# Output projection of a hybrid decoder layer by seven block products instead of eight, with the sums of weight blocks made in DRAM by adding transfers

## The chip, the cores and the metric

The kernel runs on one core of a Trainium2 chip. The metric is the device time in microseconds (us) of one execution; the median of 3 executions of the kernel before is 2147.32 us (2146.45 to 2153.07). Engines are named as in the profile: PE is TensorE's matmuls and PEld its weight loads, DVE is VectorE, ACT is ScalarE, POOL is GpSimd, SP is SyncE (here it only issues transfers).

## The reference

One decoder layer for 1024 tokens of width 2048: a norm, one input projection to 7776 columns, a group of gated-delta-rule heads and a group of sparse-attention heads that read its columns, and then the part that the change is about. The two groups' gated outputs are put side by side (2048 columns) and go through one output projection, with a residual add and a last norm:

```
o_a = rms_norm(o_a, gdn_norm_g[l]).reshape(b, t, GDN_W) * jax.nn.silu(gz)
...
o_b = dsa_sparse_attention(q_b, k_b, v_b, q_i, k_i, w_i, k_sel) * jax.nn.silu(az)
mixed = jnp.concatenate([o_a, o_b], axis=-1).astype(x.dtype) @ w_out[l]
x = x + mixed
...
return rms_norm(x, final_norm_g)
```

`mixed` is a product of a 1024 x 2048 matrix with a 2048 x 2048 matrix, in float32.

## The kernel before

Every large product is done in float32r from a high and a low part of each operand: three matmuls (high x high, high x low, low x high) for one product of tiles. A weight tile is loaded as float32 (`wraw`), rounded by ACT into `whi`, and the remainder is written to `wlo` by a subtract.

The order of work: a norm and transposition of x into 8 tiles `hT` (16 KB a partition each, 8 buffers of one tag); input projection slabs of 256 columns (`slab_cm`, banks `cm`, 192 matmuls of 512 columns each, 8 weight pieces of 256 KB a slab, `wlo` written by POOL at L195); beside the slabs run, as side work of lower priority, the indexer, the top-k search, attention (`attend`) and the delta rule. The slabs for k, q and v are followed by those for the gates (`proj_gate`), which write `szT` to DRAM; attention and the delta rule write `oT`. A list `per_piece` holds small functions; each weight piece 1 to 5 of a slab pops one and runs it behind the piece's split. In the kernel before the list holds 17 functions that make decay tables (`decay_units`).

The output projection comes last. For each half of the tokens (`hf`, 512 tokens), `mix` loads `oT` and `szT` for a k-tile of 128 rows, multiplies them (`mt`, L1233, DVE), rounds the product (L1234, ACT) and takes the remainder (L1238, DVE). Then for each 512 columns `c`, 16 weight pieces of 128 x 512 (`w_piece_k`, loaded on POOL's queue at L227, `wlo` by DVE at L232) are each used in 12 matmuls (4 token tiles x 3) into 4 banks `to` (L1309). The first half does 4 such column groups, the second 3; the last 512 columns of the second half go as two groups of 256 columns (`tm` at L244 and `tl` at L1336). `add_x` adds x to a finished bank (L1266), squares it with a running sum on ACT (L1270) and multiplies by the last norm's gain (L1272). `finish_rows` makes the row factor and scales and stores the rows. The tiles of this stage take over the 8 buffers of `hT` as the last gate slab lets them go.

Instructions are put in order by a scheduler that simulates a timeline, with priorities: weight pieces first (`P_W`), then evacuations and mixes (`P_EV`), side work (`P_SIDE`), matmuls of slabs last (`P_MM`). Each engine then runs its own list in that order, and so do the transfer queues of SP, POOL and ACT: an instruction that waits holds all behind it on its engine.

Of the kernel before, what the change touches and what calls it, by code (L numbers as in the profile page):

```python
# [22 lines left out]
P = 128  # L23
# [29 lines left out]
def hybrid_layer(ctx: ExitStack, tc, x, positions, attn_norm_g, w_in, conv_w, a_log, dt_bias,  # L53
# [139 lines left out]
    def w_split(whi, wlo, raw, ncol, eng):  # L193
        ins = S.activation(whi[:, :, :ncol], raw[:, :, :ncol], AF.Copy)  # L194
        eng.tensor_tensor(wlo[:, :, :ncol], raw[:, :, :ncol], whi[:, :, :ncol].bitcast(F32), op=ALU.subtract)  # L195
        return ins

    def w_piece(srcs, p, ncol, w2d, keep=False, into=None):

        with pri(P_W):  # L200
            raw = wp.tile([P, KPP, CG], F32, tag="wraw", name="wraw")
            o = 0
            for c0, n in srcs:
                (G if w2d is w_out else SP).dma_start(raw[:, :, o:o + n],
                                              w2d[p * KPP * P:(p + 1) * KPP * P, c0:c0 + n].rearrange("(k p) c -> p k c", p=P))
                o += n
# [8 lines left out]
            ins = w_split(whi, wlo, raw, ncol, V if w2d is w_out else G)  # L215
            if per_piece and 1 <= p <= 5:
                per_piece.pop(0)(ins)
        return whi, wlo

    last_w = []  # L220

    def w_piece_k(kt, c0):

        with pri(P_W):
            shape = [P, 2 * CG]
            raw = wp.tile(shape, F32, tag="wraw", name="wraw")
            G.dma_start(raw, w_out[kt * P:(kt + 1) * P, c0:c0 + 2 * CG])  # L227
# [3 lines left out]
            last_w[:] = [S.activation(whi, raw, AF.Copy),  # L231
                         V.tensor_tensor(wlo, raw, whi.bitcast(F32), op=ALU.subtract)]  # L232
# [891 lines left out]

    def decay_units():
# [3 lines left out]
        def load(c, g):  # L1129
            def fn(ins):  # L1130
                E[c, g] = gcp[0].tile([P, 4, P], F32, tag="gce", name="gce", bufs=2)
                SP.dma_start(E[c, g], gcrow[c * HEADS + 4 * g:c * HEADS + 4 * g + 4, :][None, :, :].to_broadcast([P, 4, P]))
            return fn

        def make(c, g):
            def fn(ins):
# [10 lines left out]
        def slot(n):  # L1147
            def fn(ins):
                if n < len(units):
                    load(*units[n])(ins)  # L1150
                if n > 0:
                    make(*units[n - 1])(ins)
# [10 lines left out]
    with tc.tile_pool(name="atp", bufs=1, reuse_waits="tile") as atp:  # L1163
        attention(atp, kvp)
# [36 lines left out]
    mtp = ctx.enter_context(tc.tile_pool(name="mtp", bufs=2, side="right", reuse_waits="tile"))  # L1201
# [6 lines left out]

    op = ctx.enter_context(tc.tile_pool(name="op", bufs=1, reuse_waits="tile"))

# [3 lines left out]
    ORDER = (4, 5, 6, 7, 0, 1, 2, 3)  # L1214
    mx = {}
    last_ox = [None]

    def mix(hf, q, ks, behind=None):

        tsl = slice(hf * HT, (hf + 1) * HT)  # L1220
        if (hf, q) not in mx:
            if hf == 1 and q in (2, 3):
                mx[hf, q] = op.tile([P, 4, 2, HT], F32R, name=f"mx1_{q}")
            else:
                mx[hf, q] = bigt(f"mx{q}", [P, 4, 2, HT], F32R)
        for k in ks:
            hi, lo = mx[hf, q][:, k, 0, :], mx[hf, q][:, k, 1, :]
            for t, src in ((hi, oT), (lo, szT)):
                ld = SP.dma_start(t.bitcast(F32), src[:, 4 * q + k, tsl])
                if last_ox[0] is not None:  # L1230
                    after(ld, last_ox[0])
            m = mtp.tile([P, HT], F32, tag="mt", name="mt", bufs=1)
            mul = V.scalar_tensor_tensor(m, hi.bitcast(F32), 0.5, lo.bitcast(F32), op0=ALU.mult, op1=ALU.mult)  # L1233
            rnd = S.activation(hi, m, AF.Copy)  # L1234
            if behind is not None:
                after(rnd, behind[0])
                after(mul, behind[1])
            V.tensor_tensor(lo, m, hi.bitcast(F32), op=ALU.subtract)  # L1238

    turn_k = itertools.count()  # L1240
    KTS = [p * KPP + k for p in ORDER for k in range(KPP)]
    fg = None
    for hf in range(2):
        NL = D - hf * CG
        with pri(P_EV):
            if hf == 0:
                for q in (2, 3, 0, 1):
                    mix(0, q, range(4 if q != 1 else 2))
            ys = [bigt(f"y{i}", [P, 2, D]) for i in range(2)]
            ss = gp.tile([P, 4, 5], F32, tag="oss", name="oss", bufs=2)  # L1250
            nss = {}
            if hf == 0:
                fg = bigt("fg", [P, D])
                SP.dma_start(fg, final_g[None, :].to_broadcast([P, D]))

        def m_ap(kt, part, sl):
            return mx[hf, kt // 4][:, kt % 4, part, slice(sl.start - hf * HT, sl.stop - hf * HT)]

        def add_x(ps, b0, nb, c0, c1):

            w = c1 - c0
            xr = op.tile([P, nb, w], F32, tag="ox", name="ox", bufs=2)
            t0 = (4 * hf + b0) * P
            last_ox[0] = SP.dma_start(xr, x[t0:t0 + nb * P, c0:c1].rearrange("(b p) c -> p b c", p=P))
            y = ys[b0 // 2][:, b0 % 2:b0 % 2 + nb, c0:c1]
            V.tensor_tensor(y, ps, xr, op=ALU.add)  # L1266
            for j in range(nb):
                jk = sdt("oj")
                n = nss.setdefault((b0 + j, c0), sum(k[0] == b0 + j for k in nss))
                S.activation(jk[:, :w], y[:, j, :], AF.Square, accum_out=ss[:, b0 + j, n:n + 1])  # L1270
            if c1 <= NL:
# [99 lines left out]
```

## Time and profile before

| | |
|---|---|
| median of 3 executions | 2147.32 us |
| profiled execution's own time | 2149.51 us |
| its span (first to last instruction) | 2147.7 us |
| mean granted TensorE clock | 0.992 of full speed |
| PE busy | 2079.6 us (97%) |
| DVE, ACT, POOL busy | 60%, 41%, 30% |

The time of an execution is its span and some 2 us around it. PE is busy nearly throughout, so a busy share by engine tells little by itself: what a stage lasts is read from stretches of the span, from the gaps of PE in them, and from the chain of waits.

### The profile page before, as it was taken

What the parts mean: (1) busy time and instruction counts of PE and PEld (TensorE: products, weight loads), DVE (VectorE), ACT (ScalarE), POOL (GpSimd) and SP (SyncE); (2) the same over time, 40 slices, a digit from 0 to 9 for tenths busy, and PEclk for the clock granted to TensorE, in tenths of its full rate; (3) what the DMA queues carried; (4) which work ended last, traced back from release to release, by engine and by line L of the source; (5) the groups of instructions that cost most, each with busy time, mean ns of one, the idle gap of its engine ahead of it and who ended that gap; (6) DMA issues with size and microseconds to landing.
All of it is one profiled execution on the core that took longest, in us unless ns stands there. A gap on an engine that the chain in (4) does not pass through costs nothing.

```text
span 2147.7 us, 30435 instructions
## 1 busy us (share of the span) xinstructions
PE 2079.6 (97%) x10529; PEld 1749.6 (81%) x10529; DVE 1298.4 (60%) x2798; ACT 872.0 (41%) x2054; POOL 642.2 (30%) x696
## 2 busy tenths in 40 slices
PE   7999999999999999999999998999999999999998
PEld 7888888877787788888888886778888887777888
DVE  8626766899999756555554479930453344445335
ACT  7425544433123555555544442122554323334223
POOL 6433334556532211222211122222322221121111
PEclk9999999999999999999999999999999999999999
DMA  6222223343224444222222242255665364556434
GB/s 190 72 74 77 74 77 79 110 129 118 86 73 113 142 116 120 81 77 85 76 63 72 70 104 59 78 163 164 182 181 147 103 235 132 168 162 230 134 120 159
DMA packets 263627, 252.08 MB, mean 117 GB/s; under 512 B 66688, under 2 KB 213552, under 8 KB 262896
## 3 DMA queue, kind: packets, MB, share of 16 engines
q1 hardware_dynamic: 210032, 188.25, 29.9%
q0 software_dynamic: 10240, 33.56, 5.1%
q10 hardware_dynamic: 43200, 28.32, 4.4%
q8 instruction: 83, 1.36, 0.3%
q14 instruction: 72, 0.59, 0.1%
HBM read 185.66 MB, written 64.39 MB: 116 GB/s over the span
## 4 chain that ended last, share of the span: by engine, by line
PE 51%; DVE 8%; DMA 5%; issue 2%; ACT 1%; SPq 1%; POOL 0%; DVEq 0%; ACTq 0%; POOLq 0%
PE cm L292 26%; PE to L1309 12%; PE lgp L148 3%; DVE ut L947 2%; PE po L148 2%; DVE mb L949 2%; PE pT L151 1%; DMA gcd<-gcrow 1%; DMA mx<-szT 1%; PE tl L1336 1%; PE tm L244 1%; PE ctok L151 1%; DVE cy L714 1%; DMA ox<-in_x_dram 1%; PE hh L923 0%
## 5 line engine op out<-in xcount | busy, mean ns | idle before, releaser
L292 PE MATMUL cm<-hT,whi 128*128 128x512 f32 (+1 forms) x3776 | 1205.6, 395 | 6.4 <-DVE sz L1121 5.7
L292 PEld LDWEIGHTS cm<-hT,whi 128*128 128x128 f32 (+1 forms) x3776 | 706.4, 188 | 151.0 <-DVE sz L1121 6.6
L292 PE MATMUL cm<-hT,wlo 128*128 128x512 f32 (+1 forms) x1888 | 746.5, 395 | 8.7 <-POOL wlo L195 8.7
L195 POOL TENSOR_TENSOR wlo<-wraw,whi 128x512 fp32r<-128x512 f32 (+1 forms) x248 | 337.3, 1361 | 902.6 <-ACT whi L194 840.3
L292 PEld LDWEIGHTS cm<-hT,wlo 128*128 128x128 f32 (+1 forms) x1888 | 355.6, 188 | 85.0 <-POOL wlo L195 14.3
L194 ACT ACTIVATE whi<-wraw 128x512 fp32r<-128x512 f32 (+1 forms) x256 | 158.7, 620 | 366.0 <-PE cm L292 252.6
L1309 PE MATMUL to<-whi,mx 128*128 128x512 f32 x896 | 279.8, 393 | 2.3 <-ACT whi L231 1.6
L1309 PEld LDWEIGHTS to<-whi,mx 128*128 128x128 f32 x896 | 167.9, 188 | 43.2 <-ACT whi L231 2.4
L664 DVE TENSOR_SCALAR_CACHE_REDUCE tj<-score,cand 128x384 bf16<-128x384 f32 (+2 forms) x198 | 187.1, 945 | 6.4
L1309 PE MATMUL to<-wlo,mx 128*128 128x512 f32 x448 | 174.7, 392 | 2.9 <-DVE wlo L232 2.9
L232 DVE TENSOR_TENSOR wlo<-wraw,whi 128x512 fp32r<-128x512 f32 x112 | 76.8, 690 | 143.1 <-ACT whi L231 143.0
L519 DVE SCALAR_TENSOR_TENSOR score<-rl,wi,score 128x512 f32<-128x512 f32 (+3 forms) x150 | 127.9, 862 | 29.5 <-ACT rl L511 22.8
L227 POOL DMA_DIRECT2D wraw<-in_w_out_dram x112 | 60.3, 539 | 252.4 <-DVE wlo L232 233.5
L231 ACT ACTIVATE whi<-wraw 128x512 fp32r<-128x512 f32 x112 | 70.1, 629 | 157.1 <-PE to L1309 124.8
L714 DVE SCALAR_TENSOR_TENSOR cy<-xr,convw,cy 128x512 f32<-128x512 f32 x144 | 118.4, 822 | 22.5 <-ACT cy L712 20.1
L832 DVE CUSTOM_DVE_ANT_0 lg<-lgp,mk 128x512 f32<-128x512 f32 (+3 forms) x96 | 53.1, 554 | 83.5 <-PE lgp L148 83.2
L1309 PEld LDWEIGHTS to<-wlo,mx 128*128 128x128 f32 x448 | 84.0, 188 | 22.4 <-DVE wlo L232 3.8
L851 DVE TENSOR_TENSOR pT<-pT 128x512 fp32r<-128x512 f32 (+1 forms) x80 | 49.7, 633 | 63.3 <-ACT pT L850 62.9
L511 ACT ACTIVATE rl<-isc 128x512 f32<-128x512 f32 (+1 forms) x105 | 59.0, 571 | 55.7 <-PE isc L148 30.2
L1121 DVE SCALAR_TENSOR_TENSOR sz<-sz,cm 128x512 f32<-128x512 f32 x32 | 21.7, 682 | 90.8 <-ACT sz L1120 90.2
L148 PE MATMUL lgp<-kT,qaT 128*128 128x512 f32 (+3 forms) x288 | 70.4, 353 | 3.9 <-ACT qaT L814 3.9
L148 PE MATMUL po<-pT,vv 128*128 128x256 f32 x432 | 72.7, 287 | 0.0
(282 smaller groups left out, 2671.1 us busy)
## 6 DMA issues: line engine op xcount, KB each, us to landing
wraw<-in_w_in_dram SPq DMA_DIRECT2D x232, 256.0 KB, 2.8
wraw<-in_w_out_dram POOLq DMA_DIRECT2D x128, 256.0 KB, 3.2
xt<-in_x_dram SPq DMA_DIRECT2D x32, 256.0 KB, 3.3
szT<-sz SPq DMA_DIRECT2D x32, 256.0 KB, 2.6
mx<-oT SPq DMA_DIRECT2D x32, 256.0 KB, 5.5
mx<-szT SPq DMA_DIRECT2D x32, 256.0 KB, 5.7
ox<-in_x_dram SPq DMA_DIRECT2D x30, 256.0 KB, 3.6
iqr<-iqT SPq DMA_DIRECT2D x48, 128.0 KB, 2.9
```

What stands on the lines that cost most here:

```text
L148: return anchored(PE.matmul(*a, **k))
L194: ins = S.activation(whi[:, :, :ncol], raw[:, :, :ncol], AF.Copy)
L195: eng.tensor_tensor(wlo[:, :, :ncol], raw[:, :, :ncol], whi[:, :, :ncol].bitcast(F32), op=ALU.subtract)
L227: G.dma_start(raw, w_out[kt * P:(kt + 1) * P, c0:c0 + 2 * CG])
L231: last_w[:] = [S.activation(whi, raw, AF.Copy), V.tensor_tensor(wlo, raw, whi.bitcast(F32), op=ALU.subtract)]
L232: V.tensor_tensor(wlo, raw, whi.bitcast(F32), op=ALU.subtract)]
L292: mms.append(PE.matmul(bank[:n, :], w[:, k, g * P:g * P + n], h_ap(kt, a, slice(h * HT, h * HT + HT)), start=(p == 0 and k == 0 and i == 0 ...
L511: S.activation(rl[:, :w], ps2[:, :w], AF.Relu)
L519: V.scalar_tensor_tensor(dst, r, w1, dst, op0=ALU.mult, op1=ALU.add)
L664: V.tensor_scalar(junk[:, :(b + 1) * P], score[b], cand[:, i:i + 1], 0.0, op0=op, op1=ALU.add, accum_out=cnt[:, i:i + 1])
L714: V.scalar_tensor_tensor(y, xr[:, j:j + HT], convw[:, j, ch:ch + 1], y, op0=ALU.mult, op1=ALU.add)
L1309: PE.matmul(banks[j], m_ap(KTS[m], a, slice((4 * hf + j) * P, (4 * hf + j + 1) * P)), ws[m][w], start=(m == 0 and i == 0), stop=(m == D // ...
```

## The change

Both matrices of the output projection are cut in four blocks: tokens in two halves (512), the inner dimension in two halves (1024), output columns in two halves (1024). Instead of eight products of blocks the changed kernel makes seven, from blocks and from sums or differences of blocks, and adds their results to the four blocks of the output in a fixed order (a form of Strassen's scheme). `wo(i, j)` are blocks of W_out; `RIGHT` lists the right-hand factor of each product.

Four of the right-hand factors are sums: `wsum1` to `wsum4`, 1024 x 1024 each, in DRAM. `block_sums` puts 32 functions in `per_piece`, behind those of `decay_units`. Each issues one transfer of 1 MB (256 rows) from POOL's queue, DRAM to DRAM: 16 plain copies and 16 that add to what is at the destination. They run behind weight pieces of the k and q slabs. A transfer that reads or adds to a slice waits for the transfer that wrote it.

The left-hand factors are made in SBUF (`factor_a`): mixes of one half, or differences of mixes (`m11`, `m21`, `m22`), split in a pair of high and low tiles; there are two sets of pairs, so a product's factor is made while the one before runs. `ms12` keeps one block in DRAM for later use. `take` evacuates a finished bank: up to two DVE adds from the bank, and adds of x and products with the gain on POOL (before, DVE did these). All w_out pieces are loaded on SP's queue (before on POOL's). A product has two column groups of 512, the first in the banks of `pj`, the second in those of the side work; 16 weight pieces, each in 12 matmuls as before: 192 matmuls a product.

```diff
-    def w_piece_k(kt, c0):
+    def w_out_piece(src):
...
-            G.dma_start(raw, w_out[kt * P:(kt + 1) * P, c0:c0 + 2 * CG])
+            SP.dma_start(raw, src)
...
+    def block_sums():
+
+        R = 256
+
+        def part(dst, src, add, r):
+            def fn(ins, low):
+                sl = slice(r * R, (r + 1) * R)
+                ld = G.dma_start(wsum[dst][sl], src[sl], accum_op=ALU.add) if add else G.dma_start(wsum[dst][sl], src[sl])
+                after(ld, low)
+            return fn
+        for dst, src, add in ((1, wo(0, 0), False), (3, wo(0, 1), False), (1, wo(0, 1), True), (3, wo(1, 1), True),
+                              (2, wsum[1], False), (2, wo(1, 1), True), (4, wsum[2], False), (4, wo(1, 0), True)):
+            for r in range(HC // R):
+                per_piece.append(part(dst, src, add, r))
...
+    def gated(i, k, hf, a, dst):
+
+        hi, lo = parts(i, k)
+        kt = k + KH * (1 - a)
+        for t, src in ((hi, oT), (lo, szT)):
+            SP.dma_start(t.bitcast(F32), src[:, kt, hf * HT:(hf + 1) * HT])
+        V.scalar_tensor_tensor(dst, hi.bitcast(F32), 0.5, lo.bitcast(F32), op0=ALU.mult, op1=ALU.mult)
+
+    def split(i, k, m):
+        hi, lo = parts(i, k)
+        S.activation(hi, m, AF.Copy)
+        V.tensor_tensor(lo, m, hi.bitcast(F32), op=ALU.subtract)
...
+    def factor_a(i, k):
+
+        if i == 0:
+            gated(0, k, 0, 0, m11[:, k, :])
+            split(0, k, m11[:, k, :])
+        elif i == 1:
+            gated(1, k, 1, 0, m21[:, k, :])
+            V.tensor_tensor(m11[:, k, :], m21[:, k, :], m11[:, k, :], op=ALU.subtract)
+            split(1, k, m11[:, k, :])
...
+        elif i == 4:
+            t = temp()
+            V.tensor_tensor(t, m21[:, k, :], m22[:, k, :], op=ALU.subtract)
+            split(4, k, t)
...
+    RIGHT = (wo(0, 0), wsum[3], wo(1, 0), wsum[2], wsum[1], wo(1, 1), wsum[4])
+
+    def with_x(hf, ch, j, cs, sub=False):
+
+        xr = stage.tile([P, 3 + HT], F32, tag="xr", name="ox", bufs=4)[:, 3:]
+        t0 = hf * HT + j * P
+        SP.dma_start(xr, x[t0:t0 + P, ch * HC + cs.start:ch * HC + cs.stop])
+        y = ys[hf, ch][:, j, cs]
+        G.tensor_tensor(y, y, xr, op=ALU.subtract if sub else ALU.add)
...
+    def gain(hf, ch, j, cs):
+        y = ys[hf, ch][:, j, cs]
+        G.tensor_tensor(y, y, fg[:, ch * HC + cs.start:ch * HC + cs.stop], op=ALU.mult)
+
+    def take(i, j, c, b):
+
+        cs = slice(c * 512, (c + 1) * 512)
+        a0, a1, y1, y2 = (t[:, j, cs] for t in (acc[0], acc[1], y11, y22))
+        if i == 0:
+            S.activation(a0, b, AF.Copy)
+        elif i == 1:
+            V.tensor_tensor(a1, b, a0, op=ALU.subtract)
+        elif i == 2:
+            V.tensor_tensor(y1, b, a0, op=ALU.add)
+            with_x(0, 0, j, cs)
+            square(0, 0, j, c)
+            gain(0, 0, j, cs)
...
+        elif i == 4:
+            V.tensor_tensor(y2, b, a1, op=ALU.add)
+            V.tensor_tensor(a0, b, a0, op=ALU.add)
+            with_x(1, 0, j, cs, sub=True)
+            with_x(1, 1, j, cs)
+            square(1, 1, j, c)
+            gain(1, 1, j, cs)
...
+    def products(i, banks, js, pieces, first, last):
+        for j in js:
+            for k, (whi, wlo) in pieces:
+                hi, lo = parts(i, k)
+                for n, (a, w) in enumerate(((hi, whi), (hi, wlo), (lo, whi))):
+                    PE.matmul(banks[j], a[:, j * P:(j + 1) * P], w, start=(k == first and n == 0), stop=(k == last and n == 2))
+
+    SP.dma_start(fg, final_g[None, :].to_broadcast([P, D]))
+    prepare_a(0)
+    prepare_a(1)
+    for i in range(7):
+        for c in range(2):
...
+                got.append((k, w_out_piece(RIGHT[i][k * P:(k + 1) * P, c * 512:(c + 1) * 512])))
+                if k != KH - 2:
+                    with pri(P_MM):
+                        products(i, banks, range(NT), got, 0, KH - 1)
+                    got = []
+            for j in range(NT):
...
+                with pri(P_EV):
+                    take(i, j, c, banks[j])
+        if i + 2 < 7:
+            prepare_a(i + 2)
```

Three places in the engines' orders. First POOL in the k slabs: before, between two `wlo` subtracts of the input weights stand only small copies for the convolution (`xr`, `halo`).

```order
L195 TENSOR_TENSOR wlo<-wraw,whi 128x512 [waits DMAHW5_49,Activation_49]
L710 COPY xr<-halo 128x3 [waits DVE_49,DMAHW2_49,PE_49,Pool_49]
L195 TENSOR_TENSOR wlo<-wraw,whi 128x512 [waits DMAHW2_49,Activation_49]
L195 TENSOR_TENSOR wlo<-wraw,whi 128x512 [waits DMAHW4_49,Activation_49]
L195 TENSOR_TENSOR wlo<-wraw,whi 128x512 [waits DMAHW0_49,Activation_49]
L195 TENSOR_TENSOR wlo<-wraw,whi 128x512 [waits DMAHW6_49,Activation_49]
```

Now an adding transfer (L1137) stands behind each of five pieces of a slab, with a wait on the earlier transfer to its slice (DMASW):

```order
L195 TENSOR_TENSOR wlo<-wraw,whi 128x512 [waits DMAHW5_49,Activation_49]
L1137 DMA wsum_4549<-in_w_out_dram 256x1024 [waits DMASW2_49]
L707 COPY xr<-halo 128x3 [waits DVE_49,DMAHW1_49,PE_49,Pool_49]
L195 TENSOR_TENSOR wlo<-wraw,whi 128x512 [waits DMAHW2_49,Activation_49]
L1137 DMA wsum_4549<-in_w_out_dram 256x1024 [waits DMASW3_49]
L195 TENSOR_TENSOR wlo<-wraw,whi 128x512 [waits DMAHW4_49,Activation_49]
L1137 DMA wsum_4551<-in_w_out_dram 256x1024 [waits DMASW4_49]
L195 TENSOR_TENSOR wlo<-wraw,whi 128x512 [waits DMAHW0_49,Activation_49]
L1137 DMA wsum_4551<-in_w_out_dram 256x1024 [waits DMASW5_49]
```

A `wlo` that stood directly behind another now stands behind a transfer that may wait. Second, DVE at the end of a column group of the output projection: before, one add from each bank, the gain, and mixes between weight pieces (L232).

```order
L1266 TENSOR_TENSOR y_16516<-to,ox 128x512 [waits PE_49] x2
L1272 TENSOR_TENSOR y_16516<-y_16516,fg 128x512 [waits DMAHW1_49,Activation_49]
L232 TENSOR_TENSOR wlo<-wraw,whi 128x512 [waits DMASW1_49,Activation_49]
L1272 TENSOR_TENSOR y_16516<-y_16516,fg 128x512 [waits Activation_49]
L1266 TENSOR_TENSOR y_16517<-to,ox 128x512 [waits DMAHW0_49,PE_49]
L232 TENSOR_TENSOR wlo<-wraw,whi 128x512 [waits DMASW2_49,Activation_49]
```

Now, at the end of the fifth product's first column group, two adds from each bank (L1337, L1338), one of which waits for POOL, and between the weight pieces (L229) the remainders of the next factor (L1264):

```order
L1337 TENSOR_TENSOR m_16470<-to,acc_16466 128x512 [waits PE_49]
L1338 TENSOR_TENSOR acc_16465<-to,acc_16465 128x512 [waits Pool_49]
L1337 TENSOR_TENSOR m_16470<-to,acc_16466 128x512 [waits PE_49]
L1338 TENSOR_TENSOR acc_16465<-to,acc_16465 128x512 [waits Pool_49]
L1337 TENSOR_TENSOR m_16470<-to,acc_16466 128x512 [waits PE_49]
L229 TENSOR_TENSOR wlo<-wraw,whi 128x512 [waits DMAHW3_49,Activation_49]
L1338 TENSOR_TENSOR acc_16465<-to,acc_16465 128x512 [waits Pool_49]
L229 TENSOR_TENSOR wlo<-wraw,whi 128x512 [waits DMAHW4_49,Activation_49]
L1264 TENSOR_TENSOR pr_16461<-m_16468,pr_16461 128x512 [waits PE_49,Activation_49]
L229 TENSOR_TENSOR wlo<-wraw,whi 128x512 [waits DMAHW5_49,Activation_49]
```

The gain has left DVE's list, and the second add and the wait for POOL have come in. Third, SP's queue in the same product: loads of x that wait for POOL (`ox`, L1305) now stand among the loads of weight pieces (L224), which were on POOL's queue before.

```order
L224 DMA wraw<-wsum_4550 128x512 [waits DMAHW4_49,DVE_49]
L1305 DMA ox<-in_x_dram 128x512 [waits DMAHW0_49,Pool_49]
L1305 DMA ox<-in_x_dram 128x512 [waits Pool_49]
L1305 DMA ox<-in_x_dram 128x512 [waits DMAHW2_49,Pool_49]
L224 DMA wraw<-wsum_4550 128x512 [waits DMAHW5_49,DVE_49]
L1305 DMA ox<-in_x_dram 128x512 [waits Pool_49]
L224 DMA wraw<-wsum_4550 128x512 [waits DMAHW6_49,DVE_49]
```

The sixth and seventh weight piece of the group are issued only when POOL has let go of an `ox` buffer.

## Rows read from the trace of the kernel before

**Rows 1.** The page, part 1: busy time of PE over the span.
```profile
PE 2079.6 (97%) x10529; PEld 1749.6 (81%) x10529; DVE 1298.4 (60%) x2798; ACT 872.0 (41%) x2054; POOL 642.2 (30%) x696
```
**Rows 2.** Busy time by stretch: the k and q slabs, the output projection in two parts.
```profile
core 0: us, PE busy (x) PEld busy (x) DVE busy (x) ACT busy (x) POOL busy (x), PEclk, DMA share, GB/s
570.00:960.00 390.00, 380.31 (x1934) 319.74 (x1933) 287.59 (x688) 179.03 (x500) 98.39 (x104) 0.99 0.37 103
1776.00:2091.00 315.00, 310.13 (x1339) 250.38 (x1339) 137.68 (x248) 100.61 (x183) 60.27 (x111) 1.00 0.50 159
2091.00:2138.50 47.50, 47.00 (x390) 46.35 (x388) 26.70 (x70) 18.21 (x40) 8.52 (x12) 1.00 0.43 148
```
**Rows 3.** Groups by line, 1776 to 2091: busy us, mean ns of one, idle time before.
```profile
L1309 PE MATMUL to<-whi,mx 128*128 128x512 f32 x892 | 278.5, 393 | 2.3 <-ACT whi L231 1.6 <-DVE sz L1121 0.6
L232 DVE TENSOR_TENSOR wlo<-wraw,whi 128x512 fp32r<-128x512 f32 x110 | 75.4, 690 | 143.1 <-ACT whi L231 143.0
L1266 DVE TENSOR_TENSOR y<-to,ox 128x512 f32<-128x512 f32 x25 | 16.7, 687 | 20.8 <-PE to L1309 15.7 <-DMA ox<-in_x_dram 5.1
L204 POOL DMA_DIRECT2D wraw<-in_w_out_dram x4 | 2.9, 720 | 8.3 <-DVE wlo L232 6.3 <-DVE wlo L195 2.0
```
**Rows 4.** Chain of waits, output projection: start us, length us, what.
```profile
1832.30 33.35 PE to L1309 x144
1968.60 121.91 PE to L1309 x528
2116.66 21.80 PE tl L1336 x185
```
**Rows 5.** What PE waited for from 1776 on: us in total, times, longest us.
```profile
PE to L1309 <- DVE wlo L232: 2.9, 2, 2.4
PE to L1309 <- ACT whi L231: 1.6, 2, 0.9
PE tm L244 <- DVE wlo L195: 0.5, 1, 0.5
```
**Rows 6.** Timeline of the end: start us, length us, engine, line.
```profile
2137.81 0.64 PE L1336 MATMUL tl<-wl,mx 128*128 128x256 f32 x4
2138.49 0.42 DVE L1266 TENSOR_TENSOR y<-tl,ox 128x256 f32<-128x256 f32 x1 [1.18 <-PE tl L1336]
2139.00 0.39 ACT L1270 ACTIVATE oj<-y 128x256 f32<-128x256 f32 x1 [1.74 <-DVE y L1266]
...
2141.81 1.04 ACT L1287 ACTIVATE y<-y,rf 128x896 f32<-128x896 f32 x1 [2.30 <-DVE rf L184]
...
2142.21 0.68 DVE L1291 TENSOR_SCALAR y<-y,rf 128x896 f32<-128x896 f32 x1
...
2143.30 0.38 SPq L1292 DMA_DIRECT2D out_dram<-y  x1
```
**Rows 7.** Timeline of DVE before the output projection: two products of mixes.
```profile
1753.49 0.69 DVE L1233 SCALAR_TENSOR_TENSOR mt<-mx 128x512 f32<-128x512 f32 x1
...
1755.61 1.68 DVE L1233 SCALAR_TENSOR_TENSOR mt<-mx 128x512 f32<-128x512 f32 x1
```
**Rows 8.** Timeline of POOL at the same time.
```profile
1755.45 1.29 POOL L195 TENSOR_TENSOR wlo<-wraw,whi 128x512 fp32r<-128x512 f32 x1 [4.66 <-ACT whi L194]
```
**Rows 9.** Transfers: a queue's packets and MB; issues with KB each, us to landing.
```profile
q0 software_dynamic: 10240, 33.56, 5.1%
...
wraw<-in_w_in_dram SPq DMA_DIRECT2D x232, 256.0 KB, 2.8
...
mx<-szT SPq DMA_DIRECT2D x32, 256.0 KB, 5.7
...
PsT<-mbt SPq DMA_DIRECT2D x2, 1024.0 KB, 8.0
```
**Rows 10.** Line L195 from 570 to 960: ns min/median/max, starts; waits for it.
```profile
L195 POOL TENSOR_TENSOR wlo<-wraw,whi x53: 1262/1296/2752, 569.4 to 954.1; 128x512 fp32r<-128x512 f32 x53
...
  PE cm L292: 2.8, 4
```

More of the change, by code (lines that the diff above doesn't have):

```diff
@@ L1123, in proj_gate, with wo @@
         slab_cm([(c0, CG)], CG, ev, budget=budget)
+    HC = D // 2
+    def wo(i, j):
+        return w_out[(1 - i) * HC:(2 - i) * HC, j * HC:(j + 1) * HC]
+    wsum = {n: dr.tile([HC, HC], F32, name=f"wsum{n}") for n in (1, 2, 3, 4)}
+    def block_sums():
[10 more added lines that the diff above has]
+                per_piece.append(part(dst, src, add, r))
     def decay_units():
@@ L1209, in hybrid_layer @@
     op = ctx.enter_context(tc.tile_pool(name="op", bufs=1, reuse_waits="tile"))
+    turn_k = itertools.count()
+    KH = KT // 2
+    NT = HT // P
     def bigt(name, shape, dt=F32):
         return big.tile(shape, dt, tag="hT", name=name, bufs=8)
[L1214 to L1223, printed above, removed]
-            else:
[L1225 to L1238, printed above, removed]
@@ new lines, in hybrid_layer @@
+    pairs = [[bigt(f"pr{i}{q}", [P, NT, 2, HT], F32R) for q in range(2)] for i in range(2)]
+    acc = [bigt(f"acc{i}", [P, NT, HC]) for i in range(2)]
+    y11 = bigt("y11", [P, NT, HC])
+    m22 = bigt("m22", [P, KH, HT])
+    m11 = op.tile([P, KH, HT], F32, name="m11")
+    m21 = op.tile([P, KH, HT], F32, name="m21")
+    y22 = m21.rearrange("p k t -> p (k t)").rearrange("p (b c) -> p b c", b=NT)
+    ms12 = dr.tile([P, KH, HT], F32, name="ms12")
+    fg = op.tile([P, D], F32, name="fg")
+    ys = {(0, 0): y11, (0, 1): acc[0], (1, 0): acc[1], (1, 1): y22}
@@ new lines, in temp @@
+    def temp():
+        return op.tile([P, HT], F32, tag="mt", name="mt", bufs=2)
+    def factor_a(i, k):
[8 more added lines that the diff above has]
+            t = temp()
+            gated(2, k, 0, 1, t)
+            SP.dma_start(ms12[:, k, :], t)
+            split(2, k, t)
+        elif i == 3:
+            gated(3, k, 1, 1, m22[:, k, :])
+            V.tensor_tensor(m11[:, k, :], m22[:, k, :], m11[:, k, :], op=ALU.subtract)
+            split(3, k, m11[:, k, :])
+        elif i == 4:
+            t = temp()
+            V.tensor_tensor(t, m21[:, k, :], m22[:, k, :], op=ALU.subtract)
+            split(4, k, t)
+        elif i == 5:
+            t = temp()
+            SP.dma_start(t, ms12[:, k, :])
+            V.tensor_tensor(t, t, m11[:, k, :], op=ALU.subtract)
+            split(5, k, t)
+        else:
+            split(6, k, m22[:, k, :])
@@ new lines, in prepare_a @@
+    def prepare_a(i):
+        with pri(P_EV):
+            for k in range(KH):
+                factor_a(i, k)
+    def products(i, banks, js, pieces, first, last):
[5 more added lines that the diff above has]
+    SP.dma_start(fg, final_g[None, :].to_broadcast([P, D]))
```

179 lines of the change are left out of this document (70 added, 109 removed).

## The prediction

> **What bounds the kernel now.** I read the busy times first: PE is busy for 97% of the span [rows 1], so time can only come from PE having less to do, or be lost by PE waiting. Then the stretches [rows 2]: the output projection is 1776 to 2138.5, with PE busy 357 of 362.5 us at full granted clock, DVE 164, ACT 119, POOL 69. The gaps of PE there come to some 5 us, none over 2.4 [rows 5]. So this stage is bound by the number of matmuls. The chain of waits gives the step of one matmul: 33.35 us for 144 is 0.2316, 121.91 for 528 is 0.2309 [rows 4]. The mean of 393 ns that the groups show [rows 3] is the length of one, and neighbours overlap; it must not be multiplied by a count. The first seven column groups (1344 matmuls) take 315 us, 45.0 a group of 192 with their waits; the last 512 columns of the second half, as 384 half-width matmuls, take 47.5 us [rows 2].
>
> **What the change removes.** Seven products of 192 matmuls of the same width are 1344, just as many as the first seven groups. At the rate of those groups they take 315 us, and the stretch of 47.5 us goes. Within a weight piece nothing changes: 12 matmuls, 2.8 us of PE, against 0.69 us of DVE for its `wlo`. At the boundaries something is won: the second column group has banks of its own, so PE need not wait for an evacuation. At the undisturbed step (0.2309) seven products would be 310 us, 5 less; I keep this for the range.
>
> **The end.** After the last matmul come an add from the bank, a square, the row factor, the scaling and a store [rows 6]. The add is now 512 wide (0.69 against 0.42), the square a little longer, and ACT scales 1024 columns and then 512 where it scaled 896 while DVE did the rest. That is 0.3, 0.2 and 0.5 us: +1.
>
> **DVE and POOL in the stage.** DVE had 138 us of work in 315 [rows 2]. Now it has, at 0.69 us each [rows 3]: 112 `wlo`; 16 gated mixes, 24 differences and 40 remainders that fall inside the stage (the rest is done before it); 64 adds from banks; and 8 row factors of 2.3 us (from 2139.5 to 2141.8 [rows 6]). That is 256 x 0.69 + 18 = 195 us, 62%. POOL gets 32 adds of x and 28 gains, 60 x 1.30 [rows 10] = 78 us, where it only issued loads. By themselves both fit.
>
> But the trace shows that they get in each other's way: a product of mixes takes 0.69 us alone and 1.68 us while POOL's subtract of 1.29 us runs beside it [rows 7, 8]. This recurs at each POOL subtract of that stretch. The Trainium skill, page "SBUF — State Buffer", section "Who interferes with whom", says that a DVE instruction with two SBUF inputs contends with a GpSimd instruction that reads SBUF, and that the port pair is locked as a whole. The trace agrees, with 1 us as the price; the skill thus speaks against moving these 60 operations to POOL.
>
> Where does it matter? In the third product DVE has 16 `wlo`, 8 adds and about 20 operations on factors, 44 x 0.69 = 30.4 us, and POOL 16 x 1.30 = 20.8; together 51.2 against 45.0 of PE. In the fifth, 16 `wlo`, 16 adds and 12 on factors are again 30.4, POOL has 24 x 1.30 = 31.2; together 61.6. If nothing of the two could overlap, PE would be held 6 + 17 = 23 us. The adds from a bank read only one SBUF operand, and no row here shows that they collide; POOL's work can also run on into the sixth product, which has 8 gains. Three weight pieces are prefetched, 8 us of PE. Bounds: 0 and 23. I take 8, a third, since the remaining products have slack to take it up.
>
> **SP's queue.** w_out now comes on the queue that also carries loads of x and stores, some of which wait for POOL or ACT; what is behind them is the next weight pieces, and PE waits for those. In the fifth product two pieces stand behind loads of x that need POOL to finish up to four adds: 4 x 1.30 plus the evacuation ahead, some 7 us after the column group's end, then 3 us for the load [rows 9] and 1.3 for the split. PE needs the sixth piece 13.7 us after the group's end. It just fits, so I cost it at nothing; its cover is POOL's pace, and if POOL is slowed by half it costs some 3 us in each of two groups, which I count with the contention.
>
> **The start.** 16 mixes must be ready for two products instead of 14. Before, one `mt` buffer made each a chain of DVE, ACT, DVE; now they go to `m11` and `m21`, and DVE can run ahead. 40 operations at 0.69 are 28 us from 1741 on, done before 1776. Delta rule work lies well before. Cost 0.
>
> **The adding transfers.** 32 transfers of 1 MB, spread over the 53 weight pieces that POOL splits from 569 to 954 [rows 10], one in 7.4 us of a piece. POOL's issue costs 0.72 us for 256 rows [rows 3], 23 us of POOL, which is busy 98 of 390 [rows 2]: hidden. What isn't sure is their length. An add must wait for a transfer issued 8 or 4 pieces earlier, at least 4 x 7.4 = 30 us. Behind a POOL that waits stand `wlo` of the input weights, and behind these PE, with some 10 us of prefetch. No row shows an adding transfer. From below: queue q0 moved 33.56 MB in 5.1% of 2147.7 us, 3.3 us per MB [rows 9]. From above: the slowest landing, 256 KB in 5.7 us, is 22.8 per MB. The nearest row is a 1 MB transfer that lands after 8.0 us [rows 9]; I take 8, far under 30, so no wait. The same 16 DMA engines carry the other loads, busy 37% there [rows 2]; 32 x 3.3 to 32 x 8 us raises this to 64% or 100%. PE already waits 2.8 us for POOL's `wlo` there [rows 10]; I add 3 us for slower loads and for side work that the scheduler has put elsewhere (by some 20 matmuls, either way). Bounds -5 and +25.
>
> **Sum.** Profiled execution 2149.5 - 47.5 + 1 + 8 + 3 = 2114.0. The median of the runs shown is 2.2 lower than that execution: 2111.8, so 2112.
>
> **Rivals.**
> A, forecast: PE stays the bound and nearly a whole product is saved. 2112, own range 2098 to 2124.
> B: DVE and POOL bind in the third and fifth product. For it: 1.68 against 0.69 [rows 7], and in-order DVE with `wlo` behind adds that wait for POOL. Against it: 62% busy, lag allowed. 23 instead of 8, and 3 in each of two groups: 2112 + 21 = 2133.
> C, slower than before: the adding transfers are slow, and POOL stands at its waits. For it: the adds read two sources, no row prices them, and POOL's order has `wlo` behind each. Against it: a pace of one in 12 us on average (385 / 32) is gentle beside 8 us. With T us for an add and 8 for a copy in turn, 16 x T + 128 must exceed 385 by the 35 us gained, so it decides from T = 18.3. At 22.8 it is 493 - 385 = 108 us held, 2112 + 108 = 2220.
> D: the stretch of the slabs suffers without a full stop, from shared DMA engines and a changed order of attention, by the upper bound of 25 instead of 3: 2134.
> That the change doesn't do what it says is excluded by PE's list, which has 1344 `to` matmuls and no `tm` and `tl`.
>
> **How the numbers follow.** Chances: A 0.64, B 0.15, C 0.13, D 0.08. What a measurement can't tell from no change is 0.3%, 6.4 us: 2141 to 2154. B and D reach into it with a fifth of their chance, 0.04, and C holds 0.13 above, so faster 0.82, same 0.05, slower 0.13. The range goes from 2097 (no contention, no disturbance, the 5 us at the boundaries half won) to 2146, beyond B and D; C stays out.
>
> **What would show it.** Right: the output projection from its first to its last `to` matmul takes 315 to 325 us; PE's gaps there are few, with DVE or POOL as releaser, in the third and fifth product; POOL's adds beside DVE operations of over 1 us. The k and q slabs end at most some us later than before. B shows as gaps of PE behind `wlo` by DVE. C shows as POOL idle with a transfer to `wsum` as releaser, and gaps at `cm` behind POOL's `wlo`. The forecast is wrong if adding transfers land after over 30 us, or if PE's gaps in the stage come to over 25 us.

## The result and the profile after

The changed kernel takes 2125.7 us (median of four runs, 2120.2 to 2127.3) against 2149.0 (2146.5 to 2153.1): ratio 0.9885, 95% interval 0.986 to 0.991. It is faster by 1.15%, 23 us, where 35 were forecast.

The two profiled executions (2149.5 and 2120.2) show where the gain of 29 between them comes from, and what it cost. First the stretches, as in [rows 2]: the k and q slabs, and the output projection from its first `to` matmul to the end of its last.

```profile
core 0: us, PE busy (x) PEld busy (x) DVE busy (x) ACT busy (x) POOL busy (x), PEclk, DMA share, GB/s
570.00:960.00 390.00, 360.14 (x1816) 301.85 (x1814) 270.28 (x647) 164.48 (x463) 115.40 (x130) 0.97 0.70 179
1785.40:2107.30 321.90, 311.59 (x1344) 251.04 (x1344) 211.52 (x328) 126.15 (x233) 91.92 (x60) 1.00 0.52 173
```

The projection takes 321.9 us instead of 362.7 (1775.8 to 2138.5): -40.8. The tail behind it has 11.2 instead of 9.2: +2.0. But the first `to` matmul starts at 1785.4 instead of 1775.8: +9.6. Together -29.2. In the k and q slabs PE is busy 360 of 390 us where it was 380 [rows 2], and the DMA share has gone from 0.37 to 0.70.

What PE waited for in the output projection (us in total, times, longest), to be set beside [rows 5], and the DVE and POOL groups there with their mean ns, beside [rows 3]:

```profile
PE to L1383 <- DVE wlo L229: 9.6, 9, 2.5
PE to L1383 <- DVE sz L1118: 1.2, 1, 1.2
```
```profile
L229 DVE TENSOR_TENSOR wlo<-wraw,whi 128x512 fp32r<-128x512 f32 x102 | 93.1, 922 | 59.6 <-ACT whi L228 59.4
...
L1338 DVE TENSOR_TENSOR acc<-to,acc 128x512 f32<-128x512 f32 x8 | 5.4, 679 | 0.0
...
L1307 POOL TENSOR_TENSOR acc<-acc,ox 128x512 f32<-128x512 f32 x16 | 22.7, 1436 | 53.3 <-DVE acc L1333 31.6 <-DVE m L1337 21.7
```

`wlo` now takes 922 ns on average where it took 690 [rows 3]: the collision with POOL is there, yet PE waits only 9.6 us behind `wlo`. The adds from a bank (L1338 is one group of them) have one operand in SBUF and one in a bank; they stay at 0.67 to 0.69 us, also where POOL works beside them.

Next, what PE waited for in the k and q slabs, and the transfers on the chain of waits between 690 and 860 (start us, length us), those over 9 us, and behind them all that the chain of the kernel before has in this stretch:

```profile
PE ctok L151 <- DVE gce L733: 11.2, 2, 10.3
PE pT L151 <- DVE lg L837: 8.3, 1, 8.3
PE lgp L148 <- DVE mx L829: 4.2, 1, 4.2
PE cm L289 <- POOL wlo L195: 2.9, 4, 0.9
```
```profile
694.22 18.78 DMA mask<-mk
...
737.45 11.52 DMA qaT<-qkT
825.81 13.29 DMA qaT<-qkT
850.22 9.36 DMA qaT<-qkT
```
```profile
709.47 3.19 DMA mask<-mk
714.56 5.22 DMA qaT<-qkT
```

What DVE and ACT waited for from 570 to 960, after, and the second of these lines before:

```profile
DVE mk L688 <- DMA mask<-mk: 8.2, 1, 8.2
ACT qaT L811 <- DMA qaT<-qkT: 36.6, 12, 7.6
```
```profile
ACT qaT L814 <- DMA qaT<-qkT: 7.5, 10, 1.2
```

So PE waits for DVE, and DVE and ACT wait for transfers. A store of the mask (192 KB) lands after 21.8 us where it took 3.2; its tile `mk` has two buffers, so DVE stands for 8.2 us before it can write a further one, and behind that in DVE's list come `cy` and then `gce`, for which PE waits 10.3 us. ACT waits for loads of queries, and DVE behind ACT. POOL isn't held: PE waits for its `wlo` no longer than before [rows 10]. The transfers from W_out land after 11.1 us in the middle; eight of these 23 are plain copies, and the eight adds issued from 636 to 760, read alone, land after 11.8. q0 and the rest in this stretch, 570 to 960 (packets, MB, share of 16 engines):

```profile
q0 software_dynamic: 6383, 32.04, 35.7%
...
wsum<-in_w_out_dram POOLq DMA_DIRECT2D x23, 1024.0 KB, 11.1
...
mask<-mk SPq DMA_DIRECT2D x1, 192.0 KB, 21.8
```

Two stretches show loss and partial return: 700 to 860, and 1500 to 1765, where the delta rule runs beside the gate slabs. Before, then after:

```profile
700.00:860.00 160.00, 155.75 (x846) 0.98 0.45 124
1500.00:1765.00 265.00, 254.82 (x1499) 0.99 0.57 172
```
```profile
700.00:860.00 160.00, 135.87 (x707) 0.93 0.74 190
1500.00:1765.00 265.00, 264.61 (x1577) 1.00 0.58 177
```

The columns are length, PE busy with its matmuls, granted clock, DMA share, GB/s. 139 matmuls fewer in the first, at 160/846 us each, are 26 us lost; 78 more in the second, at 265/1499, are 14 us given back. The clock average of 0.93 stems mainly from the two 20 us slices in which PE waits 10.3 and 8.3 us (0.74 each); it is 1.00 in the four slices between 760 and 840. With the return goes a change of order: the scheduler now places the delta rule's state products some 20 slab matmuls earlier (on average behind the 5030th of 5664 instead of the 5050th).

### The profile page after: what moved, and what is told of

The parts are those of the page before. It is cut to its first block, busy times and chain, and to the rows that moved or that the text cites. A ratio compares the mean times of both kernels' runs of the same rounds, so it can differ in the third digit from the quotient of the medians.

```text
span 2118.5 us, 29832 instructions
## 1 busy us (share of the span) xinstructions
PE 2030.4 (96%) x10145; PEld 1702.0 (80%) x10145; DVE 1350.0 (64%) x2830; ACT 882.0 (42%) x2070; POOL 685.2 (32%) x660
## 3 DMA queue, kind: packets, MB, share of 16 engines
q0 software_dynamic: 6784, 33.56, 7.0%
## 4 chain that ended last, share of the span: by engine, by line
PE 47%; DVE 10%; DMA 8%; issue 1%; ACT 1%; SPq 1%; ACTq 0%; POOL 0%; DVEq 0%
PE cm L289 25%; PE to L1383 10%; DVE ut L944 3%; DVE mb L946 2%; PE po L148 2%; PE lgp L148 2%; DMA pr<-szT 2%; DMA qaT<-qkT 2%; PE pT L151 1%; DMA mask<-mk 1%; DVE wlo L229 1%; DVE pr L1264 1%; DVE cy L711 1%; PE pv L920 1%; PE hh L920 1%
## 5 line engine op out<-in xcount | busy, mean ns | idle before, releaser
L195 POOL TENSOR_TENSOR wlo<-wraw,whi 128x512 fp32r<-128x512 f32 (+1 forms) x248 | 339.3, 1369 | 888.7 <-ACT whi L194 864.6
L289 PEld LDWEIGHTS cm<-hT,wlo 128*128 128x128 f32 (+1 forms) x1888 | 355.3, 188 | 84.3 <-POOL wlo L195 13.2
L194 ACT ACTIVATE whi<-wraw 128x512 fp32r<-128x512 f32 (+1 forms) x248 | 153.6, 619 | 338.4 <-PE cm L289 236.4
L1383 PE MATMUL to<-whi,pr 128*128 128x512 f32 x832 | 257.5, 391 | 1.8 <-DVE sz L1118 1.2
L1383 PEld LDWEIGHTS to<-whi,pr 128*128 128x128 f32 x832 | 156.1, 188 | 36.4 <-DVE sz L1118 1.6
L1383 PE MATMUL to<-wlo,pr 128*128 128x512 f32 x416 | 163.2, 395 | 9.6 <-DVE wlo L229 9.6
L711 DVE SCALAR_TENSOR_TENSOR cy<-xr,convw,cy 128x512 f32<-128x512 f32 x144 | 123.1, 855 | 19.8 <-ACT cy L709 18.4
L229 DVE TENSOR_TENSOR wlo<-wraw,whi 128x512 fp32r<-128x512 f32 x104 | 94.4, 917 | 59.6 <-ACT whi L228 59.4
L228 ACT ACTIVATE whi<-wraw 128x512 fp32r<-128x512 f32 x104 | 64.6, 626 | 100.3 <-PE to L1383 58.5
L1383 PEld LDWEIGHTS to<-wlo,pr 128*128 128x128 f32 x416 | 78.1, 188 | 31.9 <-DVE wlo L229 14.7
L713 ACT ACTIVATE xr<-cy 128x512 f32<-128x512 f32 x48 | 30.3, 631 | 103.5 <-DVE cy L711 90.2
## 6 DMA issues: line engine op xcount, KB each, us to landing
wsum<-in_w_out_dram POOLq DMA_DIRECT2D x24, 1024.0 KB, 11.1
```

The costliest lines, as they stand in the source:

```text
L195: low = eng.tensor_tensor(wlo[:, :, :ncol], raw[:, :, :ncol], whi[:, :, :ncol].bitcast(F32), op=ALU.subtract)
L289: mms.append(PE.matmul(bank[:n, :], w[:, k, g * P:g * P + n], h_ap(kt, a, slice(h * HT, h * HT + HT)), start=(p == 0 and k == 0 and i == 0 ...
L711: V.scalar_tensor_tensor(y, xr[:, j:j + HT], convw[:, j, ch:ch + 1], y, op0=ALU.mult, op1=ALU.add)
L1383: PE.matmul(banks[j], a[:, j * P:(j + 1) * P], w, start=(k == first and n == 0), stop=(k == last and n == 2))
```

## Experiments

Theory at the outset: the projection came out as forecast, and the missing 12 us were lost because adding transfers keep the DMA engines busy where attention loads and stores just in time. Rivals: the changed order of instructions alone, the bytes alone, or POOL and DVE colliding. Ratios are to the kernel before, with 95% intervals.

**Without the transfers** (the block sums aren't made; the products read blocks of W_out in their place, so the output differs).

```
-        block_sums()
-    RIGHT = (wo(0, 0), wsum[3], wo(1, 0), wsum[2], wsum[1], wo(1, 1), wsum[4])
+    RIGHT = (wo(0, 0), wo(0, 1), wo(1, 0), wo(1, 1), wo(0, 1), wo(1, 1), wo(1, 0))
```


> The changed kernel without the 32 transfers to DRAM: the four right-hand factors that were sums are read from blocks of W_out instead, so what these products compute is not the output projection; all other work is left. Theory 1 (the transfers fill the DMA engines in the k and q slabs, and loads of masks and queries land late there): the 22 us that the slabs lose go, of which some had been given back later anyway; 2103 to 2112 us. Rival (the loss is none of the transfers', it is the attention's new order or chance): 2120 to 2126. For the output projection both expect 320 to 323 us, as it was.

2113.8 us, 0.9835 (0.9814 to 0.9856), just above the expected window. The loss between 700 and 860 is gone, and so is the return later; the order of attention and delta rule is that of the kernel before again, so this run alone doesn't part the transfers from the order. The projection missed the 320 to 323 us that both sides expected: in the profiled execution, the slowest of the four, it is 325.9, with a granted clock of 0.91 in the slices 1859 to 1879 and 1959 to 1979, in which PE waits 2.5 and 4.0 us. PE in the two stretches:

```profile
700.00:860.00 160.00, 155.21 (x848) 0.99 0.46 126
1500.00:1765.00 265.00, 255.95 (x1502) 0.99 0.56 173
```

**All 32 as plain copies** (the sums are left out; the order of PE's instructions is the changed kernel's).

```
-                ld = G.dma_start(wsum[dst][sl], src[sl], accum_op=ALU.add) if add else G.dma_start(wsum[dst][sl], src[sl])
+                ld = G.dma_start(wsum[dst][sl], src[sl])
```


> The changed kernel with all 32 transfers as plain copies (16 of them no longer add, so four right-hand factors are not the sums); the order of all instructions is the same. Theory 1 with bytes as the price: an add reads twice and writes once, so 16 adds and 16 copies move 80 MB and 32 copies 64 MB; a little of the loss goes, 2119 to 2124 us. Theory 1 with the adding itself as the price: the late landings go, 2105 to 2115. Rival (order of the attention): 2125, as the changed kernel.

2106.3 us, 0.9809 (0.9792 to 0.9825): 16 (by the ratios) to 19 us (by the medians) less than with adds, for the same bytes written and in the same order. The transfers from 570 to 960, and then PE in the two stretches:

```profile
q0 software_dynamic: 6784, 33.56, 27.6%
wsum<-in_w_out_dram POOLq DMA_DIRECT2D x24, 1024.0 KB, 7.8
```
```profile
700.00:860.00 160.00, 150.37 (x803) 0.98 0.68 200
1500.00:1765.00 265.00, 264.86 (x1558) 1.00 0.58 177
```

A copied MB takes 0.276 x 390 / 33.56 = 3.2 us of all 16 engines; with half of them adds the mean is 0.357 x 390 / 32.04 = 4.3, so an added MB takes some 5.5. The loss is a third, the return stays. So the order alone isn't what costs, and the adding costs most.

**The transfers in the kernel before**, their results unused.

```
+        block_sums()
         attention(atp, kvp)
```


> The kernel before with the 32 transfers put behind its weight pieces and with nothing else changed; their results are not used. Theory 1: the slabs lose up to 22 us; 2158 to 2172 us. Rival (no loss by the transfers): 2147 to 2152.

2161.6 us, 1.0067 (1.0047 to 1.0088), as the theory expected: 13 us above the kernel before in the same comparison. The same waits of PE, 570 to 960, come without the seven products:

```profile
PE ctok L151 <- DVE gce L736: 7.1, 2, 6.2
PE pT L151 <- DVE lg L840: 6.0, 1, 6.0
PE lgp L148 <- DVE mx L832: 4.6, 1, 4.6
```

**Adds of x and gains on DVE.**

```
-        G.tensor_tensor(y, y, xr, op=ALU.subtract if sub else ALU.add)
+        V.tensor_tensor(y, y, xr, op=ALU.subtract if sub else ALU.add)
-        G.tensor_tensor(y, y, fg[:, ch * HC + cs.start:ch * HC + cs.stop], op=ALU.mult)
+        V.tensor_tensor(y, y, fg[:, ch * HC + cs.start:ch * HC + cs.stop], op=ALU.mult)
```


> The changed kernel with the 32 adds of x and the 28 products with the gain on DVE instead of POOL. If the two engines' collisions cost more than DVE's time (a weight piece's remainder takes 0.92 us in place of 0.69): remainders back at 0.69 to 0.72 us, PE's gaps behind them from 9.6 us to under 5, 2118 to 2123 us. Rival (DVE as the bound): 60 x 0.69 = 41 us more DVE, gaps grow, 2126 to 2135.

2125.1 us, 0.9895 (0.9876 to 0.9914): between its two expectations and not told apart from the changed kernel. Its `wlo`, with who waited for it (us, times):

```profile
L229 DVE TENSOR_TENSOR wlo<-wraw,whi x104: 677/691/697, 1788.3 to 2083.1; 128x512 fp32r<-128x512 f32 x104
...
  PE to L1383: 7.6, 6
```

The collision is gone (691 ns), and the projection is 319.3 instead of 321.9 us, but PE still waits 7.6 us for `wlo`. The collisions were worth 2.6 us of it; most of the wait is DVE's own queue. And the tail behind the last `to` is 12.8 instead of 11.2 us, so that of the 2.6 only 1.0 is left: too little to be told from no change.

**Later: from q0, and from v1.** `block_sums()` is called ahead of the fifth of the eight k and q slabs, or ahead of the second v slab.

```
-        block_sums()
...
         for n, (nm, i) in enumerate(slabs):
+            if n == 4:
+                block_sums()
```


> The same 32 transfers, issued one per weight piece from slab q0 on instead of from k0 on, so they run behind q0 to v1. Theory (the loss of 20 us comes from the transfers meeting the first attention units in k2, k3 and q0, where query, mask and transposes are loaded just in time): in k2 to q0 no loss against the kernel before, mask stores back to 2 to 4 us, first product of the output projection at about 1778 to 1784 us, total 2111 to 2120 us. Rival 1 (the harm is the same wherever in the attention slabs the transfers lie): the 20 us appear in q0 to v1, total 2124 to 2136 us. Rival 2 (the order that the scheduler gives the delta rule's products decides the total more than the transfers): the order of the delta rule is that of the kernel without sums, so the idle time of some 9 us between 1500 and 1775 us is back, which the changed kernel had lost.

2128.9 us, 0.9908 (0.9891 to 0.9925): rival 1 holds, and so does the sign of rival 2, since from 1500 to 1765 PE is busy only 256.4 of 265 us. 700 to 860 loses nothing now (846 matmuls), but the first `to` starts at 1796.5. Transfers on the chain from 930 on:

```profile
936.27 11.75 DMA qaT<-qkT
...
1011.25 12.46 DMA qaT<-qkT
1085.36 13.06 DMA qaT<-qkT
```

```
-        block_sums()
...
+    block_sums()
     for i in range(1, 4):
         proj_conv("v", C_GV + i * CG, 2 * i)
```


> The same 32 transfers, issued from slab v1 on, after the last attention unit, so they run behind v1 to az3. Theory (attention suffers, plain slabs do not): PE waits on attention's products as in the kernel without sums, total 2109 to 2118 us. The scheduler here puts the delta rule's products some 70 slab products later than in the changed kernel; if the order of the delta rule is what saves or costs idle time in the gate slabs, TensorE's idle time between 1500 and 1775 us is over 9 us and the total at the upper end or above, 2115 to 2125 us. Rival (any 32 adding transfers cost their 20 us wherever they run): 2125 to 2135 us.

2121.9 us, 0.9874 (0.9855 to 0.9892): above the theory's window and inside the second one, but not for its reason. Plain slabs suffer too: one store of tokens from a single buffer (median 2.3 us in the kernel before) is on the chain for 27, and PE waits behind it, and then for a load of `P2T`, where it was 0.6 us before (below, chain and waits). From 1500 to 1765 PE is busy 263.6 us although the delta rule lies later in the order, so being earlier isn't the whole reason for the return.

```profile
1255.25 26.89 DMA tokv<-tt
```
```profile
PE ctok L151 <- ACT tt L756: 12.2, 1, 12.2
PE x L976 <- DMA P2T<-PsT: 9.0, 2, 6.5
```

**Half the density**, one transfer after every second weight piece, k0 to v3.

```
                 per_piece.append(part(dst, src, add, r))
+                per_piece.append(lambda ins, low: None)
```


> The same 32 transfers from the same start, one after every second weight piece instead of every one, so they run behind k0 to v3 at half the density. Theory (the transfers delay attention's own stores and loads by keeping the 16 DMA engines busy; at half the density the DMA share between 660 and 860 us falls from 0.75 to about 0.6, as with plain copies): mask stores land in 6 to 12 us, loss in k2 to q0 of 3 to 9 us instead of 22, and the delta rule has the changed kernel's order, so the idle time in the gate slabs stays away: total 2104 to 2114 us. Rival (the loss goes by the bytes added, whenever they go): the loss is only stretched over more slabs, 2121 to 2128 us.

2116.5 us, 0.9842 (0.9824 to 0.9859), a little above the expected window. The mask stores land after 7 us at most, as expected, but the loss, 84 matmuls or 16 us (762 from 700 to 860), though below the 26 of the changed kernel, isn't the expected 3 to 9: a store of tokens (`tokk`) is on the chain for 17 us, and loads of queries for 9 and 12. With the additions on DVE as well:

> The half-density transfers and also the additions of x and the gains on VectorE instead of GpSimd. Theory: the two parts add up; the lower weight half's subtraction falls from 0.92 to 0.69 us, the output projection is 2 to 3 us shorter, total 2 to 3 us below the half-density kernel: 2101 to 2112 us. Rival (VectorE's longer queue in the tail takes it back): within 1 us of the half-density kernel or above it.

2113.3 us, 0.9833 (0.9817 to 0.9848): 3.2 us less by the medians, 2 by the ratios, with intervals that overlap, so the two aren't told apart. The traces have the projection 2.4 us shorter (321.2 against 323.6, first to last start) and the tail longer (12.9 against 11.1).

**Early: from the first index-query slab on**, where PE waited for no transfer; then with the additions on DVE.

```
+            block_sums()
             for cslab in range(4):
                 iq_slab(cslab)
...
-        per_piece.extend(slot(n) for n in range(len(units) + 1))
+        per_piece[:0] = [slot(n) for n in range(len(units) + 1)]
...
-        block_sums()
```


> The same 32 transfers, one per weight piece, issued from the first index-query slab on, so that most of them run between 110 and 440 us, where the kernel before has a DMA share of 0.28 to 0.36 and TensorE waits 4.6 us in all, none of it for a transfer. The decay units keep their slots in the four query and key slabs; the transfers left over go behind them. Theory (revised after the runs from q0 and from v1: the adding transfers cost time wherever a store or load with one or two buffers lies on the chain, and nothing where none does): first product of the output projection at 1765 to 1778 us, since the delta rule keeps the changed kernel's early order and no slab loses; total 2098 to 2112 us. Rival (32 adding transfers cost some 20 us of the span wherever they run): the loss shows up between 110 and 600 us, total 2120 to 2130 us.

> The early transfers and the additions of x and the gains on VectorE instead of GpSimd. Theory: the subtraction of the lower weight half takes 0.69 instead of 0.92 us, the output projection is 2 to 4 us shorter as in the half-density pair: total 2095 to 2110 us, 2 to 4 us below the early kernel. Rival: within 1 us of it or above.

2145.5 us, 0.9988 (0.9975 to 1.0001), and 2144.6, 0.9985 (0.9973 to 0.9997): the theory failed on both, and the first rival too, by another 15 us. In the pair the rival of the second holds: 0.9 us less, the projection 2.9 shorter and the tail again longer (12.9 against 11.1). The gain is eaten, the first `to` starts at 1814.7. PE from 110 to 440 and the waits there, before, then early:

```profile
110.00:440.00 330.00, 328.13 (x1480) 1.00 0.30 83
ACT qT L497 <- DMA iqr<-iqT: 34.8, 11, 7.3
```
```profile
110.00:440.00 330.00, 298.81 (x1308) 0.95 0.60 146
ACT qT L516 <- DMA iqr<-iqT: 74.1, 14, 14.2
PE isc L148 <- DVE qT L517: 19.4, 3, 9.3
```

The loss lies here: 172 matmuls, 38 us. That PE didn't wait for a transfer there had been read as slack. ACT did, by up to 7.3 us, and one link further PE now waits 19.4 us for `qT`. The order of the index products changed a little with it; no run parts the two.

**Shorter pieces**, 256 columns of all rows instead of 256 whole rows: 1 KB instead of 4 KB in a row.

```
-                sl = slice(r * R, (r + 1) * R)
+                sl = (slice(None), slice(r * R, (r + 1) * R))
```


> As the changed kernel, from k0 on and one per weight piece, but each of the 32 transfers takes 256 columns of all 1024 rows of a block instead of 256 whole rows: the same bytes and the same number of transfers, in pieces of 1 KB instead of 4 KB and more. Theory 1 (a small store's packets each stand behind one packet of an adding transfer on its DMA engine, so the length of the packets sets the lateness): the mask stores of 192 and 160 KB land in 5 to 9 us instead of 20, the loss in k2 to q0 falls below 10 us, total 2105 to 2115 us. Theory 2 (the time that the adding takes of the 16 engines sets it, whatever the packet length): the mask stores stay at 15 us and more and the total within 2120 to 2130 us, above that if shorter packets make the adding dearer.

2132.8 us, 0.9940 (0.9921 to 0.9959): worse than the changed kernel by 7 us and more; theory 1 is out by its time. The adds issued from 636 to 760 land after 13.3 us instead of 11.8. The Trainium skill, page "DMA: Bandwidth & Descriptors", section "Queues, rings and completion order", says that each DMA engine takes turns between its queues packet by packet. By that a small store would get past a long transfer sooner if the packets are shorter, and they are (19293 on q0 from 570 to 960, where 6383 moved as much). The stores agree in part: those of 192 and 160 KB land after 13.7 and 13.2 us instead of 21.8 and 19.8, but the next two, of 128 and 96 KB, after 10.0 and 7.0 instead of 2.7 and 2.5, and loads of queries are on the chain for 10 and 13 us, much as in the changed kernel. Neither theory's landing time came (5 to 9, or 15 and more); the total is theory 2's, with dearer adds.

**Half the length at the same density**, 64 transfers of 512 KB, one per weight piece, against the kernel with 32 of 1 MB, one per second piece (both with the additions on DVE).

```
-        R = 256
+        R = 128
-                per_piece.append(lambda ins, low: None)
```


> As the half-density kernel with the additions on VectorE, but 64 transfers of 512 KB, one per weight piece, instead of 32 of 1 MB, one per second piece: the same bytes over the same slabs k0 to v3, in bursts half as long. Theory (a store or load that comes while an adding transfer runs waits for what is left of it, so the length of a burst sets the lateness at the same mean DMA share): the chain's late transfers fall from 9 to 17 us each to 5 to 9, the loss in k2 to q0 from 15 to some 8 us, total 2103 to 2110 us. Rival (the mean share of the engines sets it, the length of a burst does not): same as the half-density kernel within 3 us, 2110 to 2117 us.

2106.2 us, 0.9805 (0.9791 to 0.9818), within the theory's window and the fastest kernel that makes the sums: 41 us below the kernel before in the same comparison, and 6 (by the ratios) to 7 (by the medians) below the half-density one. From 570 to 960 q0 takes 20.2% of the engines, against 20.0% with 1 MB. Transfers on the chain from 700 to 860, 1 MB, then 512 KB, those over 5 us from 715 on:

```profile
761.72 8.19 DMA qaT<-qkT
805.20 9.96 DMA qaT<-qkT
...
826.04 10.54 DMA qaT<-qkT
841.10 9.85 DMA L2s<-gce
```
```profile
803.94 5.42 DMA qaT<-qkT
...
822.78 7.04 DMA qaT<-qkT
837.43 6.81 DMA qaT<-qkT
```

And PE in that stretch, in the same order:

```profile
700.00:860.00 160.00, 145.33 (x770) 0.97 0.65 158
```
```profile
700.00:860.00 160.00, 156.17 (x846) 1.00 0.67 163
```

At the same share of the engines nothing is lost any more, so the length of one transfer counts, beside the share. The order of instructions hardly explains it: it differs by fewer than ten slab matmuls between the two, and the kernel with rows of 1 KB has nearly this order and 707 matmuls here. The first `to` starts at 1769.4, 6.4 us earlier than before the change.

## Why the prediction was right, and which term was too small

**The product that goes.** -47.5 and +8 for DVE and POOL, -39.5, against -40.8 measured: right. 1344 matmuls in 321.9 us lie in the announced 315 to 325, and the gaps are few, behind DVE's `wlo`, and most of their time is in the third and fifth product. The 8 us stood for collisions; moving POOL's work away gave back 2.6 us, 2.4 in the half-density pair (from 323.6 to 321.2, first to last start) and 2.9 in the early pair (322.6 to 319.7), and lost 1.6 to 1.8 of it again in the tail. The rest stayed as PE's wait for `wlo` behind other work on DVE. Size right, cause a third.

**The end.** +1, measured +2.0. **SP's queue and the start** at 0: no wait for a load is on PE's list in the projection, and the first `to` waits 1.2 us behind `sz`. Right to about that. But here too a wait can stand one link further: in the projection DVE waits 24 us for loads of factors and ACT 40 us for weight pieces, and a wait of DVE of 2.7 us stands just ahead of PE's gap of 1.4 us at 1835, one of ACT of 4.1 us just ahead of its longest, 2.5 us at 1979. What such loads cost isn't separated.

**Rival B** didn't come (9.6 us behind DVE, not 23). **Rival C** neither: adds land after 11.8 us, below its 18.3, and no wait of POOL for a `wsum` shows.

**The adding transfers** are the mis-sized term: +3, where the first `to` came 9.6 us later in the profiled execution; that execution was the fastest of the four, the median is 5.5 us above it. By the medians the transfers cost 12 us against the kernel without them, and 13 in the kernel before. Gross it is 26 us, rival D's mechanism at its full size of 25, of which some 14 returned. Two steps failed. The landing of 8 us was a copy's; as copies they do land after 7.8, but adds after 11.8 and at 5.5 us of the engines per MB instead of 3.2. And the transfers were only weighed against POOL's own waits and the weight loads, not against stores and loads with one or two buffers on the attention's chain, of which the mask stores landed 17 and 19 us late and loads of queries were on the chain for 9 to 13. The sign that the k and q slabs end at most some us later failed with it. The term's bounds, -5 and +25, held it, and so did the range; but 2125.7 lies above A's own range (2098 to 2124), and that it isn't near 2140 is luck: no term foresaw a return of 14 us. The changed order of attention, which stood in rival D as a loss, shows no loss that isn't made up: copies in that order lose 8 us (43 matmuls) from 700 to 860 and still end 7 us below the kernel without transfers.

The Trainium skill, page "DMA: Bandwidth & Descriptors", section "Rules for kernel authors", says that transfers issued from different engines run on the same 16 DMA engines and interleave. The trace agrees: the mask store goes by SP's queue and the adds by POOL's, and it landed after 21.8 us instead of 3.2.

What stays open: why the gate slabs gain. From 1500 to 1765 PE is busy 261 to 265 of 265 us in the ten kernels that have the delta rule earlier and not in the three kernels with its old place (255 to 256), but the kernel with it later than ever had 263.6 as well; no run changed that order alone. It isn't a mere catching up on time lost earlier: the kernel with 512 KB transfers, which lost nothing from 700 to 860, has 262.4 there, and the one from q0, which lost 21 us, has 256.4. Nor is it separated whether an add hurts by its engine time or by its time in flight.

## What to carry to other kernels

A transfer in the background is priced by what else is just in time: look along the chain, at every engine and not only at the bound one, for stores and loads with one or two buffers, and ask what 10 us more on each would do. If background traffic can't be avoided, thin it out and cut it into shorter transfers before looking for a quieter place. Here half the rate gave 9 us, and half the length at that rate 6 to 7 more, while moving the transfers gave, by the ratios, between 2 us less (from v1) and 22 more (early).

## What the runs showed of the hardware

- An accumulating transfer between DRAM buffers takes some 5.5 us of all 16 DMA engines per MB, a copy 3.2; landing of 1 MB 11.8 against 7.9 us, both issued from 636 to 760.
- Beside them small stores land late: 192 KB landed after 21.8 us beside adds, 9.4 beside copies, 3.0 with neither.
- Rows of 1 KB instead of 4 KB made adds slower (13.3 against 11.8 us) and POOL's issue dearer (median 1.27 against 0.86 us).
- At half the rate, adds issued from 740 to 945 land after 7.3 us with 512 KB and after 10.7 with 1 MB, the mask store of 192 KB after 4.9 and 6.1.
- A subtract on DVE with both inputs in SBUF takes 0.69 us, and up to 1.79 beside POOL's adds; an add with one input in a bank takes 0.67 to 0.69 with and without them.
